# x transposed as it lands, its reciprocal root spread by a diagonal matmul, and the first weight products taken k by k: the start of a hybrid transformer block

## The chip, the cores and the metric

The kernel runs on one core of a Trainium2 chip. The metric is the time of one execution on the device, in microseconds (us), lower is better. The core has TensorE (PE, the matrix engine; PEld is its loading of weights), VectorE (DVE), ScalarE (ACT), GpSimd (POOL) and SyncE (SP, which issues most of the DMAs). Each engine works through a list of its own in order; semaphores between the lists make one wait for another. On-chip data lie in SBUF, 128 partitions wide; matmuls write into PSUM.

## The reference

One layer of a block for 512 latent tokens (x) and 256 context tokens (ctx), each with 1024 channels. Only the first lines of it are touched by the change; the rest is cut to its outline.

```python
mod  = split(silu(c)     @ w_mod + b_mod, 6)          # c: (1, 1024), w_mod: (1024, 6144)
modc = split(silu(c_ctx) @ w_mod + b_mod, 6)
h  = rmsnorm(x,   norm1_g) * (1 + mod[1])  + mod[0]    # rmsnorm: x * rsqrt(mean(x*x) + 1e-6) * g
hc = rmsnorm(ctx, norm1_g) * (1 + modc[1]) + modc[0]
u, uc = split(h @ w_in, ...), split(hc @ w_in, ...)
y = mlstm(u, uc), diff_attention(u, uc), mamba2_ssd(u, uc)   # three branches
x = x + mod[2] * ((sum of sigmoid(gate_b) * (y_b @ w_b)) @ w_out)
x = x + mod[5] * conv_ffn(rmsnorm(x, norm2_g) * (1 + mod[4]) + mod[3])
```

## The kernel before

**Products in three parts.** The matmuls of the projections take numbers in the fp32r form. To keep the precision, each operand is split into hi (the rounded value) and lo (the remainder), and a product is the sum of three: hi x hi, hi x lo, lo x hi. `split` (L170) does it for weights: ScalarE casts hi (L173), then VectorE, or in every third call GpSimd, subtracts to get lo (L85 is the helper `tt` that issues it). `wpiece` (L177) loads 1024 x 128 numbers of a weight into `wr` (two buffers) and splits them into `wh` and `wl` (four buffers each). `proj_part` (L194) issues the matmuls for some of the eight blocks k of 128 channels: per k, three for the latents (512 columns) and, where wanted, three for the context (256 columns). L82 is the helper `mm`, L88 `stt` (two operations on two tensors and a column), L94 `ts` (on one tensor and one or two columns), L104 `act`.

**The start.** c, the norm gains, x and ctx land first (`xs`: six tiles of 128 tokens by 1024 channels). NG (L251) is the copy of the norm gains. Then, for three pairs of token tiles (L256 on): ScalarE squares and sums each (`junk`, `ssq`), VectorE computes the reciprocal root of two columns (`rs`; L121, twelve small operations), scales both tiles of xs by it, and TensorE transposes (L266); the PSUM results are copied into `xT` (channels on partitions, 768 token columns: 256 of the context, then 512 latents), half by VectorE (L270), half by ScalarE.

**The two channel parts.** `h_part(n)` makes h for four of the eight channel blocks. It loads eight pieces `wm` of w_mod (512 KB each, SP's queue, buffers set by `bufs`) and multiplies them by `scl` (the silu of c and c_ctx), four matmuls per piece: a w_mod group. The sum goes to `msb` (L338), TensorE transposes it (L341), VectorE adds the bias to get MT (shift and scale) and makes the columns A = (1 + scale) * norm gain. Then per k, for latents and context: ScalarE writes hi = A * xT + shift (`hl_101`), VectorE the same in full precision into xT in place, and VectorE (even k) or GpSimd (odd k) lo = xT - hi (`hl_102`). `hct` holds both halves for the context.

**The early pieces.** `first` (L372) lists four: the gates' columns (`wgh`, `wgl`), the keys' first piece (C_KM) and two query pieces (C_QM and the next). `early(n)` (L357) issues their matmuls for the four k of part n, piece after piece. `run` (L151) interleaves two generators in the given ratio as the program is written; the rest of the order comes from a scheduler that follows priorities by that order. After the start come the three branches, the merge and the FFN; their code is the same before and after.

```python
        run(h_part(0))
        with tc.issue_after(last[0].ins):
            for e in first[1:2]:
                e[0] = wcol(e[3])
        for n in range(1, NS):
            run(h_part(n), NK + EX, early(n - 1), KW * (NE + 1))
        run(early(NS - 1))
```

Of the kernel before, what the change touches and what calls it, by code (L numbers as in the profile page):

```python
# [18 lines left out]
P = 128  # L19
D = 1024  # L20
# [18 lines left out]
def build(tc, a, out):  # L39
# [44 lines left out]
    def tt(eng, o, x, y, op):  # L84
        eng.tensor_tensor(out=o, in0=x, in1=y, op=op)  # L85
# [129 lines left out]
    NS, NE, EX = 2, 3, 3  # L215
# [14 lines left out]
    with pool("ph0", 1) as p0:  # L230
# [25 lines left out]
        for i in range(3):  # L256
            for t in (2 * i, 2 * i + 1):
                junk = p0.tile([P, D], mybir.dt.bfloat16, tag="junk", name="junk", bufs=1)
                act(junk, xs[:, t, :], AF.Square, accum=ssq[:, t:t + 1])
            rstd(rs[:, 2 * i:2 * i + 2], ssq[:, 2 * i:2 * i + 2], 2, 1.0 / D)  # L260
            for t in (2 * i, 2 * i + 1):
                ts(V, xs[:, t, :], xs[:, t, :], rs[:, t:t + 1])
            for k in range(0, NK, 2):
                tp = pss()
                for n in range(4):
                    PE.transpose(out=tp[:, n * P:(n + 1) * P], in_=xs[:, 2 * i + n % 2, (k + n // 2) * P:(k + n // 2 + 1) * P],  # L266
                                 identity=ident)
                o = xT[:, k:k + 2, i * 256:(i + 1) * 256]
                if k % 4:
                    V.tensor_copy(o, tp.rearrange("p (k c) -> p k c", k=2))  # L270
                else:
                    S.copy(o, tp.rearrange("p (k c) -> p k c", k=2))

# [48 lines left out]
        split(wgh, wgl, wg)  # L322
        def h_part(n):
# [10 lines left out]
            if n == 0:  # L334
                pt(0)
# [14 lines left out]
            for k in range(n * KW, (n + 1) * KW):  # L350
                for r, cs, h_ in ((0, slice(TC, NT), hlat), (1, slice(0, TC), hctx)):
                    hins[0] = act(h_[0][:, k, :], xT[:, k, cs], AF.Identity, scale=A1[:, k, r:r + 1], bias=MT[:, 0, k, r:r + 1])
                    ts(V, xT[:, k, cs], xT[:, k, cs], A1[:, k, r:r + 1], MT[:, 0, k, r:r + 1], ALU.mult, ALU.add)
                    tt(G if k % 2 else V, h_[1][:, k, :], xT[:, k, cs], h_[0][:, k, :].bitcast(F32), ALU.subtract)
            yield

        def early(n):  # L357

            for i, e in enumerate(first):
                if n == 0 and i:  # L360
                    for e_ in first[i + 1:i + 2]:
                        with tc.issue_after(last[0].ins):
                            e_[0] = wcol(e_[3])
                if n == 0:
                    e[1] = (psl if e[4] else pss)()
                    e[2] = (psl if e[4] else pss)() if e[5] else None
                for k in range(n * KW, (n + 1) * KW):
                    with tc.issue_after(last[1].ins) if n < NS - 1 else ExitStack():
                        proj_part(e[0], e[1], e[2], range(k, k + 1))
                    yield  # L370

        first = [[(wgh, wgl), None, None, 0, True, True], [None, None, None, C_KM, True, True],  # L372
                 [None, None, None, C_QM, False, False], [None, None, None, C_QM + P, False, False]][0:NE + 1]
        hins = [None]
        run(h_part(0))
        with tc.issue_after(last[0].ins):
            for e in first[1:2]:
                e[0] = wcol(e[3])
        for n in range(1, NS):
            run(h_part(n), NK + EX, early(n - 1), KW * (NE + 1))  # L380
        run(early(NS - 1))
# [7 lines left out]
        with tc.issue_after(hins[0].ins):  # L389
            act(gcol[:, 5:6], gcol[:, 1:2], AF.Exp)  # L390
# [880 lines left out]
```

## Time and profile before

| | us |
|---|---|
| median of 3 runs | 1126.54 (1126.38 to 1129.1) |
| the profiled execution | 1129.0 |
| its span in the trace | 1127.2 |
| TensorE busy | 1080.3 (96%) |
| VectorE busy | 720.9 (64%) |
| ScalarE busy | 472.8 (42%) |
| GpSimd busy | 282.7 (25%) |

The mean granted clock of TensorE is 0.989 of its full speed. All times in the rows below are microseconds from the start of the span of that one execution. Matmuls follow each other in a pipeline, so the time in a row of one matmul overlaps with that of the next; what a matmul costs in a dense stretch is the distance between the starts.

### The profile page before, as it was taken

To read this page: it belongs to the slowest core of one execution; us is meant where nothing else is said; L and a number is where in the kernel's file an instruction comes from. 1 tells how busy PE (TensorE), PEld (TensorE's weight loads), DVE (VectorE), ACT (ScalarE), POOL (GpSimd) and SP (SyncE) were. 2 spreads that over 40 slices of the span, in tenths; PEclk is the share of its full clock that TensorE was granted. 3 is DMA by queue.
4 is the path that set the end of the run, shared out by engine and by line. 5 is a ranking of instruction groups with operands and counts; after the bars stand their busy time and mean duration, and the time that the engine had idled before them with its cause. 6 is when DMAs were issued, how large, how long until landed. Compare 5 with 4: busy or idle time off the path is not lost.

```text
span 1127.2 us, 16645 instructions
## 1 busy us (share of the span) xinstructions
PE 1080.3 (96%) x6402; PEld 943.8 (84%) x6402; DVE 720.9 (64%) x1351; ACT 472.8 (42%) x885; POOL 282.7 (25%) x243
## 2 busy tenths in 40 slices
PE   4898999999999999999998999989999999999998
PEld 3587899988888998789987887988888888888887
DVE  6577678669645783976685647687876656651311
ACT  5456444556324333246635363333543344431110
POOL 3230001035325732630331002243221212111110
PEclk9999999999999999999998899999999999999999
DMA  8722322236425363330316112424433333322321
GB/s 295 238 59 61 97 72 57 76 89 165 130 84 175 99 179 93 91 94 20 76 31 194 57 57 86 139 72 153 150 112 100 90 108 92 97 94 94 131 94 38
DMA packets 139951, 119.41 MB, mean 106 GB/s; under 512 B 7009, under 2 KB 115912, under 8 KB 139872
## 3 DMA queue, kind: packets, MB, share of 16 engines
q1 hardware_dynamic: 139248, 118.02, 34.6%
q8 instruction: 50, 0.82, 0.3%
q0 software_dynamic: 624, 0.33, 0.3%
q14 instruction: 29, 0.24, 0.1%
HBM read 116.10 MB, written 2.23 MB: 105 GB/s over the span
## 4 chain that ended last, share of the span: by engine, by line
PE 79%; DVE 10%; ACT 3%; DMA 3%; issue 2%; POOL 2%; SPq 0%; DVEq 0%; ACTq 0%; POOLq 0%
PE pl L82 56%; PE psx L82 18%; DVE t L85 2%; PE sc L82 2%; DVE t L88 2%; DVE wl L85 1%; ACT t L104 1%; PE pl L944 1%; DMA wm<-in_w_mod_dram 1%; POOL t L85 1%; ACT wh L173 1%; POOL wl L85 1%; DMA xs<-in_ctx_dram 1%; PE psx L266 1%; DVE rs L85 0%
## 5 line engine op out<-in xcount | busy, mean ns | idle before, releaser
L85 POOL TENSOR_TENSOR wl<-wr,wh 128x1024 fp32r<-128x1024 f32 x59 | 145.1, 2459 | 621.8 <-ACT wh L173 543.5
L173 ACT CAST wh<-wr 128x1024 fp32r<-128x1024 f32 x150 | 157.6, 1051 | 276.3 <-PE pl L82 169.0
L82 PE MATMUL pl<-h,wh 128*128 128x512 f32 (+1 forms) x768 | 223.0, 374 | 3.7 <-DVE ft L88 2.5
L85 DVE TENSOR_TENSOR wl<-wr,wh 128x1024 fp32r<-128x1024 f32 x91 | 116.3, 1279 | 155.4 <-ACT wh L173 154.5
L82 PE MATMUL pl<-hl,wh 128*128 128x512 f32 x608 | 200.3, 398 | 1.2 <-ACT sga L104 0.8
L82 PEld LDWEIGHTS pl<-h,wh 128*128 128x128 f32 x768 | 141.3, 190 | 29.5 <-issue 3.1
L82 PE MATMUL pl<-wh,hl 128*128 128x256 f32 x768 | 148.7, 288 | 3.0 <-ACT t L649 3.0
L82 PE MATMUL pl<-h,wl 128*128 128x512 f32 (+1 forms) x384 | 142.8, 373 | 0.0
L82 PEld LDWEIGHTS pl<-hl,wh 128*128 128x128 f32 x608 | 113.2, 189 | 24.8 <-issue 1.3
L82 PEld LDWEIGHTS pl<-wh,hl 128*128 128x128 f32 x768 | 121.8, 191 | 4.0 <-ACT t L649 3.2
L82 PE MATMUL pl<-hl,wl 128*128 128x512 f32 x304 | 120.3, 396 | 0.0
L82 PE MATMUL pl<-wl,hl 128*128 128x256 f32 x384 | 109.5, 286 | 0.0
L82 PEld LDWEIGHTS pl<-h,wl 128*128 128x128 f32 x384 | 72.9, 190 | 12.4
L82 PEld LDWEIGHTS pl<-wl,hl 128*128 128x128 f32 x384 | 73.3, 191 | 0.6 <-issue 0.2
L88 DVE SCALAR_TENSOR_TENSOR ft<-pl,PT,ft 128x511 f32<-128x511 f32 x88 | 65.3, 744 | 5.5 <-ACT ft L104 4.2
L82 PEld LDWEIGHTS pl<-hl,wl 128*128 128x128 f32 x304 | 57.4, 189 | 11.5
L82 PE MATMUL psx<-wh,ah 128*128 128x512 f32 (+1 forms) x176 | 66.5, 379 | 0.0
L82 PE MATMUL psx<-wl,ah 128*128 128x512 f32 (+1 forms) x176 | 66.2, 376 | 0.0
L82 PE MATMUL psx<-wh,al 128*128 128x512 f32 (+1 forms) x176 | 66.2, 376 | 0.0
L85 DVE TENSOR_TENSOR al<-ft,ah 128x512 fp32r<-128x512 f32 x22 | 45.5, 2069 | 31.3 <-ACT ah L173 31.3
L82 PE MATMUL pl<-y,wh 128*128 128x512 f32 x192 | 60.2, 395 | 0.7 <-DVE t L88 0.5
L82 PE MATMUL psx<-wh,t 128*128 128x256 f32 x256 | 46.5, 282 | 1.8 <-POOL t L85 1.0
(311 smaller groups left out, 2006.4 us busy)
## 6 DMA issues: line engine op xcount, KB each, us to landing
wr<-in_w_in_dram SPq DMA_DIRECT2D x64, 512.0 KB, 4.3
wr<-in_w_up_dram SPq DMA_DIRECT2D x44, 512.0 KB, 3.7
t<-in_w_mod_dram SPq DMA_DIRECT2D x48, 256.0 KB, 4.6
wr<-in_w_down_dram SPq DMA_DIRECT2D x22, 512.0 KB, 3.6
wm<-in_w_mod_dram SPq DMA_DIRECT2D x16, 512.0 KB, 6.0
t<-nmd SPq DMA_DIRECT2D x24, 256.0 KB, 4.8
wr<-in_w_out_dram SPq DMA_DIRECT2D x8, 512.0 KB, 3.5
fc<-in_w_mod_dram SPq DMA_DIRECT2D x16, 256.0 KB, 4.8
```

What stands on the lines that cost most here:

```text
L82: return PE.matmul(o, l, r, start=start, stop=stop)
L85: eng.tensor_tensor(out=o, in0=x, in1=y, op=op)
L88: V.scalar_tensor_tensor(out=o, in0=x, scalar=sc, in1=y, op0=op0, op1=op1)
L104: return S.activation(o, x, f, **kw)
L173: S.copy(hi, src)
L266: PE.transpose(out=tp[:, n * P:(n + 1) * P], in_=xs[:, 2 * i + n % 2, (k + n // 2) * P:(k + n // 2 + 1) * P], identity=ident)
L944: PE.transpose(out=tp[:, t * P:(t + 1) * P], in_=p0[:, (t0 + t) * P:(t0 + t + 1) * P], identity=ident)
```

## The change

The three rounds of reciprocal root and scaling are gone. TensorE transposes xs as it landed and VectorE copies all twelve PSUM tiles out. ScalarE's squares run beside it, and one reciprocal root is taken over all six columns. `dg` holds six diagonal matrices (the identity times a column of rs each, 768 columns); a matmul of ones with `dg` puts the roots of all tokens into every partition of PSUM (`rsp`: 512 columns for the latents, 256 for the context), and ScalarE copies them to SBUF (`rsb`). In `h_part`, VectorE now makes xT * A * root in one operation (the root from PSUM in part 0, from SBUF in part 1), ScalarE adds the shift to get hi, and VectorE makes lo = (xT + shift) - hi; GpSimd has no lo any more. `pt(0)`, which transposes the bias rows, moves ahead of the root. The weights' DMA (`load`) and their split (`ready`) are apart, and the keys' split is put behind the second hi. `early` takes gates and keys together, k by k, then the two query pieces. The parameter loads and the gates' split, which stood behind the transposes, stand ahead of them.

```diff
-        for i in range(3):
-            for t in (2 * i, 2 * i + 1):
-                junk = p0.tile([P, D], mybir.dt.bfloat16, tag="junk", name="junk", bufs=1)
-                act(junk, xs[:, t, :], AF.Square, accum=ssq[:, t:t + 1])
-            rstd(rs[:, 2 * i:2 * i + 2], ssq[:, 2 * i:2 * i + 2], 2, 1.0 / D)
-            for t in (2 * i, 2 * i + 1):
-                ts(V, xs[:, t, :], xs[:, t, :], rs[:, t:t + 1])
-            for k in range(0, NK, 2):
-                tp = pss()
-                for n in range(4):
-                    PE.transpose(out=tp[:, n * P:(n + 1) * P], in_=xs[:, 2 * i + n % 2, (k + n // 2) * P:(k + n // 2 + 1) * P],
-                                 identity=ident)
-                o = xT[:, k:k + 2, i * 256:(i + 1) * 256]
-                if k % 4:
-                    V.tensor_copy(o, tp.rearrange("p (k c) -> p k c", k=2))
-                else:
-                    S.copy(o, tp.rearrange("p (k c) -> p k c", k=2))
...
+        for i in range(3):
+            for t in (2 * i, 2 * i + 1):
+                junk = p0.tile([P, D], mybir.dt.bfloat16, tag="junk", name="junk", bufs=1)
+                act(junk, xs[:, t, :], AF.Square, accum=ssq[:, t:t + 1])
+            for k in range(0, NK, 2):
+                tp = pss()
+                for n in range(4):
+                    PE.transpose(out=tp[:, n * P:(n + 1) * P], in_=xs[:, 2 * i + n % 2, (k + n // 2) * P:(k + n // 2 + 1) * P],
+                                 identity=ident)
+                V.tensor_copy(xT[:, k:k + 2, i * 256:(i + 1) * 256], tp.rearrange("p (k c) -> p k c", k=2))
+        pt(0)
+        rstd(rs, ssq, 6, 1.0 / D)
+        dg = p0.tile([P, 6, P], F32, name="dg")
+        tt(V, dg, ident.unsqueeze(1).broadcast_to([P, 6, P]), rs.unsqueeze(2).broadcast_to([P, 6, P]), ALU.mult)
+        rsp = [pss(), pss()]
+        mm(rsp[0], ones.broadcast_to([P, P]), dg[:, 2:6, :].rearrange("p t c -> p (t c)"))
+        mm(rsp[1][:, 0:TC], ones.broadcast_to([P, P]), dg[:, 0:2, :].rearrange("p t c -> p (t c)"))
+        rsb = p0.tile([P, NT], F32, name="rsb")
+        S.copy(rsb[:, TC:NT], rsp[0])
+        S.copy(rsb[:, 0:TC], rsp[1][:, 0:TC])
...
-            if n == 0:
-                pt(0)
...
             for k in range(n * KW, (n + 1) * KW):
                 for r, cs, h_ in ((0, slice(TC, NT), hlat), (1, slice(0, TC), hctx)):
-                    hins[0] = act(h_[0][:, k, :], xT[:, k, cs], AF.Identity, scale=A1[:, k, r:r + 1], bias=MT[:, 0, k, r:r + 1])
-                    ts(V, xT[:, k, cs], xT[:, k, cs], A1[:, k, r:r + 1], MT[:, 0, k, r:r + 1], ALU.mult, ALU.add)
-                    tt(G if k % 2 else V, h_[1][:, k, :], xT[:, k, cs], h_[0][:, k, :].bitcast(F32), ALU.subtract)
-            yield
+                    rb = rsb[:, cs] if n else rsp[r][:, 0:cs.stop - cs.start]
+                    stt(xT[:, k, cs], xT[:, k, cs], A1[:, k, r:r + 1], rb, ALU.mult, ALU.mult)
+                    hins.append(act(h_[0][:, k, :], xT[:, k, cs], AF.Identity, bias=MT[:, 0, k, r:r + 1]))
+                    stt(h_[1][:, k, :], xT[:, k, cs], MT[:, 0, k, r:r + 1], h_[0][:, k, :].bitcast(F32), ALU.add, ALU.subtract)
+                if k % 2:
+                    yield
+
+        def load(e):
+
+            r = wp.tile([P, 1024], F32, tag="wr", name="wr", bufs=2).rearrange("p (k c) -> p k c", c=P)
+            nc.sync.dma_start(r, w_in.rearrange("(k p) c -> p k c", p=P)[:, :, e[3]:e[3] + P])
+            e[0] = r
+
+        def ready(e):
+            lo = wp.tile([P, 1024], F32R, tag="wl", name="wl", bufs=4).rearrange("p (k c) -> p k c", c=P)
+            hi = wp.tile([P, 1024], F32R, tag="wh", name="wh", bufs=4).rearrange("p (k c) -> p k c", c=P)
+            split(hi, lo, e[0])
+            e[0] = (hi, lo)
...
         def early(n):
 
-            for i, e in enumerate(first):
-                if n == 0 and i:
-                    for e_ in first[i + 1:i + 2]:
-                        with tc.issue_after(last[0].ins):
-                            e_[0] = wcol(e_[3])
+            ks = range(n * KW, (n + 1) * KW)
+            if n == 0:
+                for e in first[0:2]:
+                    banks(e)
+            for k in ks:
+                for e in first[0:2]:
+                    proj_part(e[0], e[1], e[2], range(k, k + 1))
+                    yield
+            for e in first[2:]:
                 if n == 0:
-                    e[1] = (psl if e[4] else pss)()
-                    e[2] = (psl if e[4] else pss)() if e[5] else None
-                for k in range(n * KW, (n + 1) * KW):
-                    with tc.issue_after(last[1].ins) if n < NS - 1 else ExitStack():
-                        proj_part(e[0], e[1], e[2], range(k, k + 1))
+                    with tc.issue_after(last[0].ins):
+                        load(e)
+                    ready(e)
+                    banks(e)
+                for k in ks:
+                    proj_part(e[0], e[1], e[2], range(k, k + 1))
                     yield
 
         first = [[(wgh, wgl), None, None, 0, True, True], [None, None, None, C_KM, True, True],
-                 [None, None, None, C_QM, False, False], [None, None, None, C_QM + P, False, False]][0:NE + 1]
-        hins = [None]
-        run(h_part(0))
+                 [None, None, None, C_QM, False, False], [None, None, None, C_QM + P, False, False]]
+        hins = []
+        hp0 = h_part(0)
+        for _ in range(NK):
+            next(hp0)
         with tc.issue_after(last[0].ins):
-            for e in first[1:2]:
-                e[0] = wcol(e[3])
-        for n in range(1, NS):
-            run(h_part(n), NK + EX, early(n - 1), KW * (NE + 1))
-        run(early(NS - 1))
+            load(first[1])
+        next(hp0)
+        with tc.issue_after(hins[1].ins):
+            ready(first[1])
+        e0 = early(0)
+        for _ in range(3):
+            next(e0)
+        run(hp0)
+        run(h_part(1), NK + 2, e0, 13)
+        run(early(1))
```

TensorE at the start of the program, before: L266 are the transposes of xs, the names `pl_289` the sum of the w_mod groups of part 0, `prm` the parameter rows of `pt(0)`, `msb` the modulation of part 0.

```order
L266 MATMUL psx<-ident,xs 128x128 x16
L82 MATMUL pl_289<-wm,scl 32x256 x12
L266 MATMUL psx<-ident,xs 128x128 x16
L82 MATMUL pl_289<-wm,scl 32x256 x8
L266 MATMUL psx<-ident,xs 128x128 x3
L82 MATMUL pl_289<-wm,scl 32x256 x4
L266 MATMUL psx<-ident,xs 128x128 x13
L82 MATMUL pl_289<-wm,scl 32x256 x4
L315 MATMUL psx<-ident,prm 128x128
L82 MATMUL pl_289<-wm,scl 32x256 x4
L341 MATMUL psx<-ident,msb 128x128 x2
```

The same place after the change; `dg,ones` are the two spreading matmuls.

```order
L314 MATMUL psx<-ident,xs 128x128 x48
L82 MATMUL pl_269<-wm,scl 32x256 x20
L297 MATMUL psx<-ident,prm 128x128
L82 MATMUL psx<-dg,ones 128x512
L82 MATMUL psx<-dg,ones 128x256
L82 MATMUL pl_269<-wm,scl 32x256 x12
L344 MATMUL psx<-ident,msb 128x128 x2
```

All 48 transposes now stand ahead of the first w_mod group; five groups follow in one piece, and three stand behind the spreading matmuls.

VectorE from the bias copy on, before: PT is the transposed bias, MT the modulation columns, A_85 the scale columns; operations on `hl_102` and on `hct` with three names are lo.

```order
L316 COPY PT<-psx 128x128
L85 TENSOR_TENSOR MT<-psx,PT 128x2x2 x4
L88 SCALAR_TENSOR_TENSOR A_85<-MT,NG 128x8
L85 TENSOR_TENSOR wl<-wr,wh 128x1024
L94 TENSOR_SCALAR xT<-xT,A_85,MT 128x512
L94 TENSOR_SCALAR xT<-xT,A_85,MT 128x256
L85 TENSOR_TENSOR hl_102<-xT,hl_101 128x512
L94 TENSOR_SCALAR xT<-xT,A_85,MT 128x512
L85 TENSOR_TENSOR hct<-xT,hct 128x256
```

VectorE at that place after the change, beginning with the diagonals.

```order
L85 TENSOR_TENSOR dg<-ident,rs 128x768
L298 COPY PT<-psx 128x128
L85 TENSOR_TENSOR MT<-psx,PT 128x2x2 x4
L88 SCALAR_TENSOR_TENSOR A_85<-MT,NG 128x8
L88 SCALAR_TENSOR_TENSOR xT<-xT,A_85,psx 128x512
L88 SCALAR_TENSOR_TENSOR xT<-xT,A_85,psx 128x256
...
L88 SCALAR_TENSOR_TENSOR xT<-xT,A_85,psx 128x512
L88 SCALAR_TENSOR_TENSOR xT<-xT,A_85,psx 128x256
L88 SCALAR_TENSOR_TENSOR hl_102<-xT,MT,hl_101 128x512
L88 SCALAR_TENSOR_TENSOR hct<-xT,MT,hct 128x256
L85 TENSOR_TENSOR wl<-wr,wh 128x1024
```

The weight split and the first lo have changed places, and all eight scalings of the part stand ahead of the first lo.

TensorE around the transposes of the second part's modulation, before: `pl_388` and `pl_389` are the gates' sums for latents and context, `pl_432` and `pl_433` the keys', `psx` from hl the query pieces'; L315 transposes the later parameter rows (`pt(1)`, `pt(2)`).

```order
L82 MATMUL psx<-hl_101,wl 128x512
L341 MATMUL psx<-ident,msb 128x128 x2
L82 MATMUL psx<-hl_101,wh 128x512
L82 MATMUL psx<-hl_102,wh 128x512
...
L82 MATMUL psx<-hl_102,wh 128x512
L82 MATMUL psx<-hl_101,wl 128x512
L315 MATMUL psx<-ident,prm 128x128 x2
L82 MATMUL pl_388<-hl_101,wgh 128x512
L82 MATMUL pl_432<-hl_101,wh 128x512
```

The same place after the change, where `pl_346` and `pl_347` are the gates' sums and `pl_348` and `pl_349` the keys'.

```order
L82 MATMUL psx<-hl_101,wl 128x512
L344 MATMUL psx<-ident,msb 128x128 x2
L297 MATMUL psx<-ident,prm 128x128 x2
L82 MATMUL pl_346<-hl_101,wgh 128x512
L82 MATMUL pl_348<-hl_101,wh 128x512
L82 MATMUL psx<-hl_101,wh 128x512 x2
L82 MATMUL pl_347<-hct,wgh 128x256
L82 MATMUL pl_349<-hct,wh 128x256
L82 MATMUL pl_346<-hl_102,wgh 128x512
```

Twelve matmuls of the fourth piece's part 0 stood behind the two transposes of msb; now all of the part 0 matmuls stand ahead of them, and the matmuls on part 1's h follow.

## Rows read from the trace of the kernel before

**Rows 1.** The page's first part: busy time, share of the span and instructions.

```profile
PE 1080.3 (96%) x6402; PEld 943.8 (84%) x6402; DVE 720.9 (64%) x1351; ACT 472.8 (42%) x885; POOL 282.7 (25%) x243
```

**Rows 2.** Windows: busy (count) of PE, PEld, DVE, ACT, POOL; clock; DMA; GB/s.

```profile
19.00:20.00 1.00, 1.00 (x17) 0.56 (x20) 0.95 (x5) 0.08 (x1) 0.00 (x0) 1.00 0.51 195
20.00:21.00 1.00, 1.00 (x19) 0.49 (x8) 1.00 (x2) 0.00 (x0) 0.00 (x0) 1.00 0.06 10
...
33.00:33.50 0.50, 0.50 (x6) 0.07 (x6) 0.50 (x2) 0.50 (x2) 0.00 (x0) 0.53 1.13 338
36.00:36.50 0.50, 0.50 (x9) 0.20 (x8) 0.50 (x2) 0.30 (x1) 0.39 (x1) 0.56 0.91 299
36.50:37.00 0.50, 0.50 (x9) 0.21 (x2) 0.50 (x2) 0.50 (x1) 0.00 (x0) 1.00 0.94 360
86.00:87.00 1.00, 0.00 (x0) 0.00 (x0) 0.00 (x0) 0.99 (x2) 0.00 (x0) 1.00 0.21 63
```

**Rows 3.** Timeline to 30: start, time, engine, operation, count, [idle before <- releaser].

```profile
11.21 0.17 DVE L251 COPY NG<-psx 128x16 f32<-128x16 f32 x1 [2.71 <-ACT scl L104]
12.24 0.17 DVE L94 TENSOR_SCALAR rs<-ssq 128x2 f32<-128x2 f32 x1 [0.86 <-ACT junk L104]
...
14.42 0.16 DVE L88 SCALAR_TENSOR_TENSOR rs<-rs,rs 128x2 f32<-128x2 f32 x1
...
19.03 1.65 PE L82 MATMUL pl<-wm,scl 128*32 128x256 f32 x24
...
25.76 1.46 DVE L270 COPY xT<-psx 128x512 f32<-128x512 f32 x2 [0.77 <-PE psx L266]
...
28.63 0.37 ACT L338 COPY msb<-pl 128x256 f32<-128x256 f32 x1 [1.96 <-PE pl L82]
...
29.82 0.15 DVE L88 SCALAR_TENSOR_TENSOR A<-MT,NG 128x8 f32<-128x8 f32 x1
```

**Rows 4.** Timeline from 34 to 89: the places that decide when TensorE goes on.

```profile
34.48 0.80 PE L82 MATMUL pl<-hl,wgh 128*128 128x512 f32 x1
...
51.57 0.38 PE L341 MATMUL psx<-ident,msb 128*128 128x128 f32 x2
...
52.27 0.16 DVE L88 SCALAR_TENSOR_TENSOR A<-MT,NG 128x8 f32<-128x8 f32 x1
...
65.78 0.27 PE L82 MATMUL pl<-hct,wl 128*128 128x256 f32 x1
...
88.87 0.39 PE L82 MATMUL pl<-wh,hl 128*128 128x256 f32 x1 [3.04 <-ACT t L649]
```

**Rows 5.** Timeline of TensorE: starts of matmuls that follow each other.

```profile
42.75 0.64 PE L82 MATMUL psx<-wm,scl 128*32 128x256 f32 x8
43.32 0.50 PE L82 MATMUL pl<-hl,wh 128*128 128x512 f32 x1
...
59.27 0.28 PE L82 MATMUL pl<-hct,wh 128*128 128x256 f32 x1
59.39 0.40 PE L82 MATMUL pl<-hl,wgh 128*128 128x512 f32 x1
59.62 0.40 PE L82 MATMUL pl<-hl,wgl 128*128 128x512 f32 x1
```

**Rows 6.** Groups by form: busy, mean ns; or min/mean/max ns and from when.

```profile
L88 DVE SCALAR_TENSOR_TENSOR t<-t,scl,t x48: 731/744/2857, 258.5 to 652.5; 128x512 f32<-128x512 f32 x48
L88 DVE SCALAR_TENSOR_TENSOR t<-pl,PT,t 128x255 f32<-128x255 f32 x20 | 9.4, 468 | 2.0 <-ACT t L104 1.9
L85 DVE TENSOR_TENSOR hl<-xT,hl 128x512 fp32r<-128x512 f32 x4 | 2.7, 681 | 0.0
L85 DVE TENSOR_TENSOR wl<-wr,wh 128x1024 fp32r<-128x1024 f32 x4 | 4.9, 1225 | 7.1 <-ACT wh L173 7.1
L82 PE MATMUL psx<-t,ones x4: 591/592/595, 305.2 to 358.1; 128*128 128x512 f32 x4
```

**Rows 7.** Timeline near 887: GpSimd and VectorE, both with two SBUF inputs.

```profile
886.82 2.40 POOL L85 TENSOR_TENSOR wl<-wr,wh 128x1024 fp32r<-128x1024 f32 x1 [8.48 <-ACT wh L173]
887.30 2.48 DVE L85 TENSOR_TENSOR al<-ft,ah 128x512 fp32r<-128x512 f32 x1 [1.88 <-ACT ah L173]
```

More of the change, by code (lines that the diff above doesn't have):

```diff
@@ L213, in proj_w @@
         return pre.pop(c0) if c0 in pre else proj_cm(wcol(c0), lat, ctxt)
-    NS, NE, EX = 2, 3, 3
+    NS = 2
     W = D // NS
@@ new lines, in ready, with banks @@
+        def ready(e):
[3 more added lines that the diff above has]
+            e[0] = (hi, lo)
+        def banks(e):
+            e[1] = (psl if e[4] else pss)()
+            e[2] = (psl if e[4] else pss)() if e[5] else None
+        def early(n):
+            ks = range(n * KW, (n + 1) * KW)
[7 more added lines that the diff above has]
+            for e in first[2:]:
+                if n == 0:
+                    with tc.issue_after(last[0].ins):
[4 more added lines that the diff above has]
+                    proj_part(e[0], e[1], e[2], range(k, k + 1))
@@ L388, in build @@
         V.tensor_copy(gcol[:, 0:5], PT[:, 2, R3_G:R3_G + 5])
-        with tc.issue_after(hins[0].ins):
+        with tc.issue_after(hins[-1].ins):
             act(gcol[:, 5:6], gcol[:, 1:2], AF.Exp)
```

## The prediction, made before the changed kernel was run

> **What bounds the kernel now.** The page's first part puts TensorE at 96% of the span [rows 1], so what the change can move is where TensorE idles, runs slowly or waits: the start, the only place that the diff touches. I read the start in the order of time (the timeline), then the same stretch cut into short windows for clock and DMA, then the waits behind it. Three things stand out. TensorE's first matmul on h lo comes at 34.48 [rows 4]; before it the scale columns A of the first channel part are ready at 29.97 [rows 3]. Between 19 and 21 the DMA engines nearly stop (195 and 10 GB/s) [rows 2]: five w_mod buffers are full and wait for TensorE. And from 33.0 to 36.4 the granted clock is 0.5, its lower level of 1.2 GHz, after a stretch in which TensorE had mostly idled; it is full again from 36.5 [rows 2]. Then TensorE is busy without a gap to the last matmul of the keys (C_KM), at 65.78, and on to 85.8. There it idles 3.04 us until 88.87 [rows 4], waiting for ScalarE; the chain of waits leads from there back through a cast, a split and a load of a later weight piece to the end of the keys, which frees that piece's buffer. So the one number that carries to the end is when the keys are done: 65.78 + 0.27 = 66.05.
>
> I walk the new order to that number. The trace is one of 1129.0 us (span 1127.2, the rest 1.8 lies outside); the median of the runs shown is 1126.54, 2.5 lower. The sum is a difference to that trace, put on the median.
>
> **1. To the scale columns of part 0.** Removed: three reciprocal roots one after another, six scalings of xs, and the split of the drains over two engines. The transposes now need only the landed x; VectorE drains all twelve. It starts after the NG copy, at 11.38, as ScalarE's order up to there is unchanged. Twelve drains at 0.73 (two took 1.46) make 8.8: 20.1. One root of twelve small operations, as before (12.24 to 14.58, 2.3): 22.5 [rows 3]. The diagonal has 768 elements, two inputs: between 0.68 for 512 and 1.23 for 1024 [rows 6], I take 0.95: 23.4. The two spreading matmuls are not in the trace; the nearest is the 512-column spread by ones, two records of 0.59 each [rows 6]. For 512 and 256 columns together that bounds them at 0.9 (records fully overlapped) and 1.8 (not at all); I take 1.3, as other records overlap: 24.7. TensorE's list has three w_mod groups queued behind them, 1.65 for three [rows 3]: 26.4. From there to A, before needs 28.63 to 29.97 plus the semaphore, 1.4: A at **27.8**, 2.2 earlier. The loads cover this: five groups run in one piece when the transposes end (eight drains, 17.2, plus some 0.6), so loads 6 to 8 are issued from about 18.3 and the hole of 19 to 21 closes. If the last of them is late, A is 0.6 later.
>
> **2. To the first lo.** All eight scalings of part 0 now stand ahead of the first lo on VectorE. None of that form (two tensors and a column) is new in kind: 0.74 for 512 [rows 6], 0.47 for 256; four of each are 4.8 end to end, 4.2 if neighbours overlap by 0.08; I take 4.4. With a lo of 0.74 TensorE starts at **33.0** instead of 34.48, 1.5 earlier. ScalarE's hi casts lie inside: its first starts after one scaling, and the weight split that stood before it is moved behind. GpSimd's lo operations fall away; that costs VectorE 4 x (0.74 + 0.47) but ends its own stalls beside GpSimd.
>
> **3. To the second transposes of the modulation.** From here TensorE is the limit, and its list decides. Spacings: 0.23 for 512 columns, 0.12 for 256, and 0.7 for a w_mod group (0.57 from the group to the next matmul, plus the gap at its edges) [rows 5]. Before: 35 of 512, 23 of 256 and 6 groups from 34.48 to 51.57 [rows 4]: 8.05 + 2.76 + 4.2 = 15.0 of 17.1; of the 2.1 left about 1.0 is the half clock up to 36.4, the rest waits. Now: 46, 22 and 5 groups: 10.6 + 2.6 + 3.5 = 16.7, since two more weight pieces' part 0 stands ahead of these transposes. With the same 2.1: 33.0 + 18.8 = **51.8**. So the 1.5 is spent: 51.8 against 51.57.
>
> GpSimd still splits one weight piece here, beside VectorE's lo of k = 2 and 3. A two-input VectorE operation beside such a split took 2.48, the split 2.40 [rows 7]; alone its kind takes 0.68 [rows 6]. So the lo of k = 2 comes some 2 later, near 39.3, and TensorE has about 6 us of matmuls between the first lo and that one, so it arrives at 39 too: I cost it at nothing, and at 1 if that cover is thinner. The Trainium skill, "GPSIMD Engine Reference", section 1 (Specifications), says the same: its SBUF interfaces are shared with VectorE and contend when VectorE has two SBUF inputs. The trace agrees (2.48 against 0.68); a reader who ignored it would have the lo of k = 2 at 37 and the same sum, but with 2 us of slack.
>
> **4. To the keys' end.** Before, twelve matmuls of the fourth piece still stand behind the second transposes (12 x 0.23 = 2.8); they cover the 0.9 to the new A (51.57 to 52.43) [rows 4] and the first hi and lo, so TensorE never waits. Now nothing stands there. From 51.8: 0.9 to A plus 0.3 for a small copy put between: 53.0; eight scalings 4.4: 57.4; another copy 0.3 and the lo of k = 4, 0.74: 58.5. Until then TensorE has only four matmuls of 512 and two of 256 that need no lo, 1.2 us; it idles about 5 of 6.7 us in two waits. Behind them stand 28 of 512 and 22 of 256: 6.4 + 2.6 = 9.1, and the later lo are done by 63, before they are wanted. Keys done at **67.6**, against 66.05: 1.5 later.
>
> **5. Behind the keys.** Sixteen matmuls of the early pieces are left instead of twelve, 0.9 more for TensorE, but it waits 3.04 at 85.83 for the chain from the keys, so that is hidden: 88.3 against a release of 88.87 + 1.5 = 90.4. The 1.5 is carried to the end. Further back the two orders differ only in how neighbours interleave; nothing prices that, and I allow 2 either way.
>
> Sum: -2.2 at A, +0.7 for the scalings (-1.5 at the first lo), +1.7 for the longer list up to the second transposes (+0.2), +1.3 for the waits less the work moved ahead: **+1.5**, so 1126.5 + 1.5 = **1128.0** (1130.5 for an execution like the profiled one). That is 0.13%, below the 0.3% (3.4 us) that a measurement of this kernel can tell from no change.
>
> **Rivals.**
> *The early start carries (faster).* If TensorE finds work in the waits of step 4, because A comes well before it reaches the transposes' end or the scalings overlap more than I think, the keys end when the work does: 33.0 + (46 + 32) x 0.23 + (22 + 24) x 0.12 + 3.5 + 2.1 + 0.5 for the transposes = 62.6, or 61.6 without the half clock: 3.4 to 4.4 earlier, **1122.6**. For it speaks that TensorE is 96% busy and all this work is the same. Against it: every engine takes its list in order, and the list has no matmul free of lo there. It decides if the two waits together are under 1 us.
>
> *The clock falls in the waits (slower).* In step 4 TensorE idles 5 of 6.7 us, and 9.1 us of dense matmuls follow. In the trace an idle stretch before 33.0 was followed by 3.4 us at half clock, worth 1.7; at 85.8 a wait of 3.04 was not (clock 1.00) [rows 2, 4]. Should the clock be down for 7 of the 9.1 us at full-clock pace, they cost up to 3.5 more: 1128.0 + 3.5 = **1131.5**. It decides from 3.8 us at half clock on (1.9 lost). The Trainium skill, "TensorE: Matmul & The Clock Gate", Part 1, has an idle TensorE at half rate until sustained activity releases it; by that rule the fall would come. The two rows disagree among themselves, so I give it less than even.
>
> *The start is not what counts.* If the 3.04 at 85.8 hangs on something that doesn't move with the keys (the gates' own chain through ScalarE's logarithms), an earlier or later end of the keys vanishes, up to 3: **1126.5**. The gates' sums end about 1 us before the keys in either order, so it would look the same: no change.
>
> **How the numbers follow.** Forecast 0.5; the start doesn't count 0.1; early start carries 0.18; clock 0.22. The first two lie within 0.3% but for the interleaving behind (2 either way), which takes 0.02 to each side; of the clock case a fifth stays within. Faster 0.2, same 0.58, slower 0.22. The range runs from the fast rival to the slow one with half of the unpriced 2: 1122.6 to 1132.
>
> **What would show it.** Right: the DMA hole at 19 to 21 gone; drains back to back from 11.4 to 20; A of part 0 near 27.8; first lo matmul near 33; second transposes near 52; then two idle pieces of TensorE, together near 5 us, and the keys done at 67 to 68; the wait at 88 shortened to 2. Wrong: no idle after the second transposes, or a granted clock of 0.5 behind them for several us; A of part 0 later than 29 (drains or the spread dearer); or a new wait of over 2 us behind 118 us, where the lists only interleave anew.

## The result and the profile after

The changed kernel takes 1136.74 us (median of 6 executions, 1133.58 to 1140.51) against 1126.88 before: a ratio of 1.0081, 95% interval 1.0062 to 1.0101. By the medians it is slower by 9.9 us, where 1128.0 and no measurable change were forecast; the time lies above the range. The profiled execution took 1136.85 us with a span of 1133.9. That of before (1129.0) is 2.1 us above this median of before, so its span of 1127.2 shows only 6.7 of the difference.

The page's first part after the change:

```profile
PE 1086.6 (96%) x6406; PEld 947.0 (84%) x6406; DVE 721.2 (64%) x1336; ACT 469.5 (41%) x881; POOL 276.2 (24%) x235
```

Windows of the changed kernel (columns as in [rows 2]):

```profile
19.00:20.00 1.00, 0.64 (x8) 0.16 (x8) 0.83 (x6) 0.00 (x0) 0.00 (x0) 1.00 1.05 399
20.00:21.00 1.00, 0.62 (x9) 0.21 (x9) 0.86 (x5) 0.00 (x0) 0.00 (x0) 1.00 1.02 395
57.00:58.00 1.00, 0.81 (x2) 0.72 (x3) 1.00 (x3) 0.98 (x2) 0.00 (x0) 0.50 0.00 0
59.00:60.00 1.00, 1.00 (x4) 0.74 (x3) 1.00 (x6) 0.10 (x1) 0.00 (x0) 0.50 0.00 0
91.00:92.00 1.00, 1.00 (x5) 1.00 (x6) 1.00 (x3) 0.21 (x2) 0.00 (x0) 0.50 0.08 16
93.00:94.00 1.00, 1.00 (x7) 1.00 (x6) 0.97 (x2) 0.00 (x0) 0.00 (x0) 0.50 0.00 0
```

The hole in the DMA is closed (399 and 395 GB/s where [rows 2] have 195 and 10). The granted clock is at its lower level near 57 to 60 and again near 91 to 94; in the kernel before it was full in both places, behind the wait at 86 too [rows 2]. Windows of the kernel before:

```profile
57.00:58.00 1.00, 1.00 (x7) 0.78 (x5) 1.00 (x3) 0.98 (x2) 0.77 (x2) 1.00 0.00 0
91.00:92.00 1.00, 1.00 (x11) 1.00 (x10) 0.97 (x3) 0.00 (x0) 0.00 (x0) 1.00 0.06 16
```

Timeline of the changed kernel up to the first lo:

```profile
11.16 7.26 DVE L316 COPY xT<-psx 128x512 f32<-128x512 f32 x12
...
18.34 0.16 DVE L94 TENSOR_SCALAR rs<-ssq 128x6 f32<-128x6 f32 x1
...
20.75 0.96 DVE L85 TENSOR_TENSOR dg<-ident,rs 128x768 f32<-128x768 f32 x1
...
21.85 1.53 PE L82 MATMUL psx<-dg,ones 128*128 128x512 f32 x4 [0.57 <-DVE dg L85]
...
26.26 0.16 DVE L88 SCALAR_TENSOR_TENSOR A<-MT,NG 128x8 f32<-128x8 f32 x1
26.53 4.29 DVE L88 SCALAR_TENSOR_TENSOR xT<-xT,A,psx 128x512 f32<-128x512 f32 x8
...
28.65 0.64 PE L82 MATMUL psx<-wm,scl 128*32 128x256 f32 x8 [2.71 <-DMA wm<-in_w_mod_dram]
...
30.74 0.75 DVE L88 SCALAR_TENSOR_TENSOR hl<-xT,MT,hl 128x512 fp32r<-128x512 f32 x1
...
32.93 0.50 PE L82 MATMUL pl<-hl,wgh 128*128 128x512 f32 x1
```

Timeline of TensorE from the second transposes on, at the rows that answer to [rows 4], and its further waits up to 401:

```profile
50.86 0.38 PE L344 MATMUL psx<-ident,msb 128*128 128x128 f32 x2
...
53.51 0.50 PE L82 MATMUL pl<-hl,wgh 128*128 128x512 f32 x1 [1.47 <-ACT hl L104]
...
57.19 0.79 PE L82 MATMUL pl<-hl,wgh 128*128 128x512 f32 x1 [2.25 <-DVE hl L88]
...
67.56 0.28 PE L82 MATMUL pl<-hct,wl 128*128 128x256 f32 x1
...
90.93 0.58 PE L82 MATMUL pl<-wh,hl 128*128 128x256 f32 x1 [2.36 <-ACT t L682]
...
120.36 1.13 PE L82 MATMUL psx<-t,kw 128*128 128x130 f32 x8 [0.64 <-DVE kw L92]
...
236.54 0.85 PE L789 MATMUL pl<-ident,t 128*128 128x128 f32 x6 [1.30 <-DVE sm L88]
264.80 0.70 PE L82 MATMUL psx<-xw,t 128*128 128x256 f32 x2 [0.92 <-POOL xw L85]
278.15 0.87 PE L789 MATMUL pl<-ident,t 128*128 128x128 f32 x6 [1.46 <-ACT t L790]
...
400.45 1.10 PE L82 MATMUL psx<-t,t 128*128 128x64 f32 x8 [0.94 <-DVE t L85]
```

The kernel before at the last five places (it has no wait at the first L756 group, near 230):

```profile
118.00 1.13 PE L82 MATMUL psx<-t,kw 128*128 128x130 f32 x8 [1.55 <-DVE kw L92]
...
257.92 0.70 PE L82 MATMUL psx<-xw,t 128*128 128x256 f32 x2 [0.20 <-POOL xw L85]
271.66 0.88 PE L756 MATMUL pl<-ident,t 128*128 128x128 f32 x6 [0.94 <-ACT t L757]
272.91 0.73 PE L82 MATMUL pl<-hl,wh 128*128 128x512 f32 x2 [0.37 <-ACT t L757]
...
394.43 1.10 PE L82 MATMUL psx<-t,t 128*128 128x64 f32 x8 [0.93 <-DVE t L85]
```

Read the two side by side as a lag. The last matmul of the keys starts 1.8 later (67.56 against 65.78), the wait for ScalarE ends 2.1 later (90.93 against 88.87), the kw matmul (the first on `kw`, at 118.00 and 120.36) 2.4 later. So behind the lower clock from 91 to 94 the lag has grown by 0.3 only: the kw matmul waits 0.64 where it had waited 1.55, and that hides most of the loss. Then comes what the prediction had no price for: from the kw matmul to the wait near 400 the kernel before needs 276.43 us and the changed one 280.09, 3.7 more, in code that the change does not touch. The waits there account for 2.2 of it (1.30 + 0.92 + 1.46 against 0.20 + 0.94 + 0.37). From 400 to the end the order of TensorE's list is the same in both kernels but for single records, and the lag grows only from 6.0 to 6.7.

So two theories stood against each other. **S**: all of it follows from the start, the late keys and the half clock behind the waits. **L**: a part comes from the later list of TensorE, which the scheduler interleaves in another way. (The lists of the other engines behind the start are laid out anew with it, so "the list" below stands for the whole layout; no run tells which engine's order costs the time.)

### The profile page after: what moved, and what is told of

It is laid out like the page before. It is cut to its first block, busy times and chain, and to the rows that moved or that the text cites. A ratio compares the mean times of both kernels' runs of the same rounds, so it can differ in the third digit from the quotient of the medians.

```text
span 1133.9 us, 16621 instructions
## 1 busy us (share of the span) xinstructions
PE 1086.6 (96%) x6406; PEld 947.0 (84%) x6406; DVE 721.2 (64%) x1336; ACT 469.5 (41%) x881; POOL 276.2 (24%) x235
## 4 chain that ended last, share of the span: by engine, by line
PE 73%; DVE 10%; issue 2%; POOL 2%; ACT 2%; DMA 1%; SPq 0%; DVEq 0%; ACTq 0%
PE pl L82 52%; PE psx L82 17%; PE sc L82 2%; DVE t L85 2%; DVE t L88 2%; POOL t L85 1%; DVE wl L85 1%; DMA t<-nmd 1%; PE pl L977 1%; ACT wh L173 0%; DVE sm L88 0%; DVE h L85 0%; DVE sm L896 0%; DVE zacc L85 0%; DVE sga L88 0%
```

## The experiments

Medians in us; the ratio is to the kernel before on the same chip. "Keys" is the start of the last keys matmul, "kw to 400" the distance just read (276.43 in the kernel before; a dash where the list begins in another order), both from the profiled execution.

| kernel | median | ratio (95%) | keys | kw to 400 |
|---|---|---|---|---|
| changed (first time) | 1136.74 | 1.0081 (1.0062 to 1.0101) | 67.56 | 280.09 |
| e4 changed, again | 1136.97 | 1.0076 (1.0051 to 1.0101) | 67.43 | 280.01 |
| e1 cover of 12 | 1129.89 | 1.0029 (1.0010 to 1.0048) | 62.64 | 279.66 |
| e2 cover of 12, other list | 1127.86 | 1.0006 (0.9989 to 1.0023) | 63.83 | 276.57 |
| e3 cover of 22 | 1124.28 | 0.9971 (0.9955 to 0.9988) | 61.96 | - |
| e5 transposes alone | 1126.35 | 0.9995 (0.9974 to 1.0016) | 63.26 | 275.83 |
| e6 early pieces alone | 1129.17 | 1.0010 (0.9992 to 1.0027) | 69.76 | - |
| e7 before, no cover | 1128.79 | 1.0017 (1.0000 to 1.0034) | 64.76 | - |
| e8 lo sooner | 1128.92 | 1.0011 (0.9995 to 1.0026) | 67.37 | - |
| e9 cover and lo sooner | 1123.74 | 0.9976 (0.9960 to 0.9992) | 61.98 | - |
| e10 waits filled (28) | 1129.88 | 1.0031 (1.0016 to 1.0046) | 66.82 | 276.42 |
| e11 filled a little (8) | 1128.89 | 1.0021 (1.0009 to 1.0034) | 66.35 | 276.58 |
| e12 filled (8), the changed list | 1134.55 | 1.0069 (1.0054 to 1.0085) | 69.27 | 280.42 |

The last column splits by order. From the kw matmul to 400 the kernel before, e2, e10 and e11 have the same order on all five engines, but for single records, and take 276.42 to 276.58. The changed kernel, e4, e1 and e12 have another, again the same on all five engines, with some 250 of TensorE's 1778 records elsewhere, and take 279.66 to 280.42. The wait of 1.30 near 236 stands in these four profiles and in none of the other ten. e5 has a third order.

**e1 to e4: cover behind the second transposes, with different later lists.** Cover is work that TensorE can do where it would wait: here matmuls on part 0, which the call of `run` fills in between the steps of `h_part(1)`. The edit is one number or two, which leave part of them behind the transposes:

```diff
-        run(h_part(1), NK + 2, e0, 13)
+        run(h_part(1), NK + 8, e0, 13)    # e1
+        run(h_part(1), NK + 4, e0, 13)    # e2
+        run(h_part(1), NK + 6, e0, 10)    # e3
```

> One number changed against the changed kernel: the fill of the second channel part is spread over 16 steps instead of 10, so that twelve matmuls of 512 columns on part 0 stand behind the second modulation's transposes, as in the kernel before. The list of TensorE from the keys on is that of the changed kernel up to its row 3288. Theory S (the loss arises at the start: two waits of 1.47 and 2.25 us and the half clock behind them, and once more behind the wait at 88): the twelve matmuls (2.8) take the place of one wait, keys done near 65 instead of 67.84, TensorE no longer at half clock near 57 or near 91, total 1136.7 - 2.8 - 1.7 - 1.7 = 1130.5, and from 118 to 284 the lead or lag against the kernel before changes by less than 1. Theory L (a part arises later, because the scheduler interleaves the matmuls between 118 and 284 in another way): the keys come earlier in the same way, but between 118 and 284 this kernel still loses 3 to 4 us against the kernel before, as the changed kernel did (2.4 behind at 118, 6.1 at 284).

> The same with 12 steps instead of 10: again twelve matmuls behind the second transposes, the start as in the run before, but the later list of TensorE stands nearer to that of the kernel before (82 matmuls moved against it, 279 against the changed kernel). Theory S: the same time as the other kernel with twelve matmuls, within 1 us. Theory L: the 3 to 4 us between 118 and 284 go, so 2 to 4 us less than that kernel: 1126.5 to 1128.5.

> 14 steps and a fill of 10: 22 matmuls of part 0 stand behind the second transposes, and the later list of TensorE is that of the kernel before from 460 matmuls behind the keys on (57 moved in all). Theory S: both waits are covered (22 x 0.23 = 5.1), the keys are done near 63, 3 earlier than before, total 1123.5 to 1125, and 1.5 to 4 less than with twelve. Theory L: the same start, and no loss between 118 and 284, so that it is 5 to 8 less than the kernel with twelve matmuls and the changed kernel's later list, 1123.

> The changed kernel once more, on the chip on which the other three run, to compare with them: 1136.7, within 2 either way by both theories; the keys done at 67.8 and the release at 91, if its first profile is typical, with half clock behind each of the two waits in most executions.

In e1 the two waits became one of 2.07, and the keys came 5 us sooner than in the changed kernel. It leads the kernel before by 1.9 at the kw matmul and has lost that lead, and 1.3 more, at 400. Timeline of e1:

```profile
53.62 0.50 PE L82 MATMUL pl<-hl,wgh 128*128 128x512 f32 x1 [2.07 <-DVE hl L88]
...
116.09 1.13 PE L82 MATMUL psx<-t,kw 128*128 128x130 f32 x8 [1.28 <-DVE kw L92]
...
395.75 1.10 PE L82 MATMUL psx<-t,t 128*128 128x64 f32 x8 [0.95 <-DVE t L85]
```

The start is repaired and 3.2 us are lost behind it all the same, with the changed kernel's list: L. But e1's total, 1129.89, is near S's 1130.5 too, though the lower clock behind the wait at 86 stayed (0.50 from 87 to 90). On this one chip the kernel before takes 1126.18, e1 1129.89 and the changed kernel (e4) 1136.97. e1 and e4 share the later list, so 7.1 hang on the start and the clock, more than on the list: both theories hold a part. e2 lies 2.0 below e1 with the keys 1.2 later, as L has it, though the two intervals overlap. e3 has the cover and the other list, and beats the kernel before. e4 repeats the changed kernel.

**e5 and e6: one half of the change each.** e5 has the changed order of the parameter loads, the transposes, the root and the scalings, with the old loading of the weights, the old `early` and the old call:

```diff
-        run(hp0)
-        run(h_part(1), NK + 2, e0, 13)
-        run(early(1))
+        run(h_part(0))
...
+        for n in range(1, NS):
+            run(h_part(n), NK + EX, early(n - 1), KW * (NE + 1))
+        run(early(NS - 1))
```

e6 is the kernel before with the changed `early`, `load`, `ready`, `banks` and that call in place of its own, and a yield behind every second block in `h_part`.

> The changed kernel's load, transposes, spread root and scalings, with the early pieces one after the other as in the kernel before: twelve matmuls stand behind the second transposes. Its later list of TensorE is a third one (179 moved against before, 324 against the changed kernel). Theory S (all is decided by the end of the keys and the clock there): the start as in the runs with twelve matmuls behind, release near 86 instead of 88.87, total 1126.2 - 2.9 + 1.7 for a half clock = 1125. Theory L (the list between 118 and 284 costs by itself): the time at the first matmul behind 284 differs from what the lead at 118 gives by more than 1, either way; total 1122 to 1129.

> The kernel before with the early pieces alone taken as in the change (gates and keys k by k, load and split apart). No matmul stands behind the second transposes, but VectorE's list has the first lo behind two scalings, not eight. Theory S: first lo near 34.5 as before, second transposes 2.8 later, near 54.4, then waits of about 0.9 and 1.0, keys near 68, 1.9 later than before: 1128, and 1130 if the clock falls there. Theory L: the same start, and up to 4 more or less between 118 and 284, since 136 matmuls of the later list stand elsewhere.

Neither half alone is measurably slower. e5's keys are 2.5 earlier than before and bring nothing that can be measured; its time is 1.4 above S's figure and inside L's wide range, so it doesn't tell them apart. Of its lead, 2.5 at the end of the wait for ScalarE (86.33), nothing is left at the kw matmul (117.96), behind a wait of 1.66. In e6 both waits behind the second transposes are short (0.40 and 0.83), but the transposes themselves start at 55.76, 1.4 later than expected, after a stretch of lower clock (0.50 from 31 on, 0.69 from 37 to 38), and the keys come at 69.76 instead of 68. The total is that of theory S; the list neither added nor took. The keys end 4.0 later than before and the total is at most 0.27% (3.0 us) higher: not all of a later end of the keys comes through to the end.

**e7 and e8: what makes the waits.** e7 changes one number of the kernel before; e8 changes VectorE's list in the changed kernel.

```diff
-    NS, NE, EX = 2, 3, 3
+    NS, NE, EX = 2, 3, 0              # e7
```

```diff
+            los = []
...
-                    stt(xT[:, k, cs], xT[:, k, cs], A1[:, k, r:r + 1], rb, ALU.mult, ALU.mult)
+                    with tc.issue_after(los[-3].ins) if n and len(los) > 2 else ExitStack():
+                        stt(xT[:, k, cs], xT[:, k, cs], A1[:, k, r:r + 1], rb, ALU.mult, ALU.mult)
...
+                    los.append(...the lo of this block...)    # e8
```

> The kernel before with one number changed (EX 3 to 0), so that all matmuls of part 0 stand ahead of the second transposes and none behind them. Theory S: the cover is what matters: two waits appear in the kernel before as well, together 2 to 3, the keys come 2 later, total 1128 to 1130. Theory L: the same, and the later list (120 moved, and not the changed kernel's) adds or takes up to 4. If neither wait appears, the cover was not what the kernel before lived on.

> The changed kernel, with VectorE's list in part 1 changed so that the lo of a block stands behind three scalings instead of eight. Still no matmul behind the second transposes. Theory S: the second wait (2.25, for the first lo) goes or falls below 0.5, the first (1.47, for the first hi) stays; the clock need not fall near 57; keys 65 to 66 instead of 67.8; total 1137 - 2 - 0 to 3.4 = 1131.5 to 1135. Theory L: the later list is another one (354 moved against the changed kernel, 184 against before), so the loss between 118 and 284 may be gone, for 1128 to 1131.

e7's total lies where it was expected, but the way there doesn't: without cover the kernel before waits only 0.40 and 0.83, where its first lo stands behind two scalings, and the keys come 1.0 sooner than before, not 2 later (its profile has no lower clock near 33). The long second wait needs the eight scalings. e8 shows the same from the other side. VectorE's timeline in e8, up to the first lo of part 1, which in the changed kernel came at 56.39:

```profile
51.98 1.81 DVE L88 SCALAR_TENSOR_TENSOR xT<-xT,A,rsb 128x512 f32<-128x512 f32 x3
53.71 0.28 DVE L298 COPY PT<-psx 128x128 f32<-128x128 f32 x1
53.91 0.74 DVE L360 SCALAR_TENSOR_TENSOR hl<-xT,MT,hl 128x512 fp32r<-128x512 f32 x1
```

The second wait is gone. Yet the keys end no sooner (67.37): behind the first wait the clock was down from 54 on (0.56, 0.50 and 0.50 in the three windows to 57), with TensorE busy throughout. With the keys where the changed kernel has them, e8 takes 8 us less; only its later list and the clock are others.

**e9: both cures.** e3's call and e8's scalings, these in both parts (`if len(los) > 2`).

> The two cures together: 22 matmuls of part 0 behind the second transposes, and the first lo of each part behind three scalings instead of eight; the later list stands near that of the kernel before (55 moved). Theory S: as the kernel with 22 matmuls alone (1124.3), less at most 0.7 at the first lo of part 0, since no wait was left in part 1: 1123 to 1125. Theory L: the same, as that list is the same from 460 matmuls behind the keys on.

As expected: no wait is left in part 1, and 0.24% less than before (0.08 to 0.40). e3's interval overlaps with it.

**e10 to e12: TensorE kept busy in the waits.** Extra matmuls write columns 256 to 511 of the keys' context sum, which nothing reads:

```diff
         run(early(1))
...
+        with tc.issue_after(tlast[0].ins):         # tlast: second transposes; e10: 12, e12: 8
+            for _ in range(12):
+                mm(first[1][2][:, 256:512], wgh[:, 0, :], hctx[0][:, 0, :], False, False)
...
+                    if dum[0] and k == 4 and n == 0 and w is not first[0][0]:   # e10: 16, e11: 8
+                        dum[0] = 0
+                        with tc.issue_after(z.ins):
+                            for _ in range(16):
+                                mm(pc[:, 256:512], wgh[:, 0, :], hctx[0][:, 0, :], False, False)
```

> The changed kernel with 28 extra matmuls of 256 columns that nothing reads, 12 in the first wait behind the second transposes and 16 in the second (1.4 and 1.9 us at 0.12 each, so that they end before the wait would): TensorE keeps busy there, and nothing that is needed comes sooner. The later list is a new one (266 moved against the changed kernel). Theory S: only the clock can gain: if it stays full near 57, the keys come at 66.2 instead of 67.8 and the total is 1137 - 1.7, with the second fall near 91 gone another 1.7: 1133.5 to 1135.5. Theory L: the loss between 118 and 284 goes with the list, another 3 to 4: 1130 to 1132. The claim that the clock falls because TensorE idles is wrong if it still falls near 57.

> The same with only 8 such matmuls, in the second wait (1.0 of 2.25 us); TensorE's list behind them is, row for row, that of the run with 28. Theory S: the waits stay, the clock falls near 57 as in the changed kernel, so 1137 within 1, and 2 to 4 more than the run with 28. Theory L: the keys as in the changed kernel (67.4 to 67.8) and yet 3 to 4 less in total, 1133, since only the later list differs.

> The changed kernel with 8 such matmuls in the first wait (1.0 of 1.87 us); here TensorE's later list is, row for row, that of the changed kernel. Theory S and theory L alike: 1137 within 1 if the clock still falls near 57; 1133.5 to 1135.5 if the shorter idle time keeps it up. Beside the run with 8 in the second wait it differs in the later list alone: theory L has it 3 to 4 slower than that one, theory S equal within 1.

e11 and e12 are the cleanest pair. They have the same start but for where the eight small matmuls and a few neighbours stand, and ran on the same chip. Timeline of e11, then of e12:

```profile
119.71 1.13 PE L82 MATMUL psx<-t,kw 128*128 128x130 f32 x8 [0.75 <-DVE kw L92]
...
396.29 1.11 PE L82 MATMUL psx<-t,t 128*128 128x64 f32 x8 [0.93 <-DVE t L85]
```

```profile
122.62 1.13 PE L82 MATMUL psx<-t,kw 128*128 128x130 f32 x8 [0.99 <-DVE kw L92]
...
239.13 0.85 PE L793 MATMUL pl<-ident,t 128*128 128x128 f32 x6 [1.30 <-DVE sm L88]
...
403.04 1.10 PE L82 MATMUL psx<-t,t 128*128 128x64 f32 x8 [0.93 <-DVE t L85]
```

e12 needs 280.42 from kw to 400, e11 276.58: 3.8 more with the changed kernel's list, with its wait at 239 again. The medians differ by 5.7. In this pair of profiles the rest arises at the start, where e12's keys come 2.9 later, with a longer stretch of lower clock, as the windows show. (Behind 400 some 70 matmuls stand elsewhere too; there e12 makes up 0.6.) First e11, then e12:

```profile
57.00:58.00 1.00, 0.92 (x4) 0.79 (x5) 1.00 (x4) 1.00 (x1) 0.00 (x0) 1.00 0.00 0
```

```profile
57.00:58.00 1.00, 0.66 (x2) 0.57 (x3) 1.00 (x3) 1.00 (x1) 0.00 (x0) 0.50 0.00 0
62.00:63.00 1.00, 1.00 (x4) 0.82 (x4) 0.00 (x0) 0.00 (x0) 0.37 (x3) 0.50 0.11 1
```

With eight matmuls in the second wait the clock stayed full and the keys came at 66.35, 1.1 to 1.2 sooner than in the changed kernel; with eight in the first wait it was down until 63 and they came at 69.27. So the fall near 57 is worth 1.1 or more. It is no theory of the whole, though: e10, with both waits filled down to 0.43 and 0.54 and the clock full near 57, was not faster than e11, and the clock still fell near 91 in both. S's figures for e10 (1133.5 to 1135.5) and e11 (1137) are refuted, and for e12 that it would equal e11 within 1. L gave 3 to 4 between e11 and e12, and 3.8 were found from kw to 400; but it had e11 at 1133, 4 too high, since it too counted on the fall near 57. Both theories had e12 at 1137 within 1 if the clock fell; it fell, and e12 took 1134.55.

## Why the prediction failed, point by point

**Steps 1 and 2** were right in their times, with compensating errors. A of part 0 was ready at 26.42, not 27.8: twelve drains took 7.26, not 8.8, and the others hold (root from 18.34, diagonal 0.96 against 0.95, spread 1.53 against 1.3). The first lo was done at 31.49, but TensorE reached it at 32.93 (33.0 forecast), as it waited 2.71 for a w_mod piece that landed no sooner and then ran at the lower clock. That the two agree is luck. The expected slowing of VectorE beside GpSimd's split didn't come (below); it had been costed at nothing.

**Step 3**: second transposes at 50.86, 51.8 forecast. The 2.1 of lower clock and waits that were carried over from before were too much: the clock was down from 29 to 33 here (0.68 to 0.50), ahead of the first lo, and full from 33 on.

**Step 4** had the mechanism and the size: two waits, 1.47 and 2.25 (and 0.40 ahead of them), together 4.1 against "about 5". The keys were done at 67.84, 67.6 forecast, and that is luck: TensorE went on from the second wait at 57.19, 1.3 sooner than forecast, and then took 10.65 for work priced at 9.1, since in this sum stood no half clock. Without it the keys would have been done 1.1 or more sooner (e11). The second wait comes from the eight scalings ahead of the lo (e8), as step 4 had it.

**Step 5** fails. The release, "88.87 + 1.5 = 90.4", was right to 0.5 (90.93). What failed is the sentence behind it: "Further back the two orders differ only in how neighbours interleave; nothing prices that, and I allow 2 either way". That list costs 3.7 between the kw matmul and 400: 279.66 to 280.42 in the four profiles that have it, 276.42 to 276.58 in the four that have the order of the kernel before. By itself this would still lie within the range (1128.0 + 3.7 = 1131.7); with the clock it does not. Nor does "The 1.5 is carried to the end" hold as a rule: of e5's lead nothing is left at the kw matmul, and e6's keys come 4.0 later for 3.0 at most.

**The rival "the clock falls in the waits"** was right that it falls near 57, which was given less than even. Its price was too high there (up to 3.5; 1.1 to 1.2 measured by e11, 1.5 by the 10.65 against 9.1), and it missed that the clock would fall more often: near 91, which in the kernel before had not come behind a longer wait, and elsewhere (below). The Trainium skill, "TensorE: Matmul & The Clock Gate", Part 1, lets the number of slow matmuls vary from one run of a kernel to the next. The executions agree (0.981 to 0.992 granted to the changed kernel), so a single profile of before was a weak ground for a price.

**The early start carries** only once the waits are covered: e3 and e9 take 1124.3 and 1123.7, where this rival had 1122.6. Of the signs of being wrong, the lower clock behind the waits came. A new wait of over 2 us behind 118 did not: the longest is 1.46, so that sign was too coarse for the loss that it was to catch. The chances and the range are also added up wrongly by their own terms, which give 0.2, 0.6 and 0.2 for faster, same and slower, and 1121.6 to 1132.5; nothing hangs on it.

The sum, then. In the two profiles the lag is 6.7: 2.4 at the kw matmul, where 1.5 had been forecast for the keys (the fall near 57 is 1.1 or more of it), 3.7 from the list, 0.7 behind 400. The other 3 of the 9.9 are not in this pair, and as an estimate they go with the clock. Executions with the same granted clock differ by 6 to 7: at 0.989 two of the changed kernel average 1133.88 and thirteen of the kernel before 1127.85; at 0.986 it is 1136.85 in one against 1129.82 in nine. And the changed kernel was granted less, 0.9835 in the median of twelve executions against 0.990 over 93. Where the lower stretches lie differs from one profile to the next. Apart from the last matmuls, the changed kernel's profile has 31 us of them: 29 to 33, 57 to 60, 91 to 94, 586 to 589, 620 to 630 and 640 to 647. That of before has 24: 33 to 36, 613 to 623, 634 to 641 and 753 to 757. The profiled execution of e4, the fastest of the changed kernel's twelve (1131.70), has 17, those near 57 and 91 among them. Why the others come and go stays open. That the list's loss comes from the waits named above (2.2 of 3.7) is read from the profiles alone, in all four that have this list; TensorE has no other wait over 0.15 between kw and 400, and where the other 1.5 arises stays open.

## What to carry to other kernels

Where a scheduler lays out the program, an edit at the start is also an edit of everything behind it. Compare the whole list of the bound engine before and after, not only the edited stretch, and try one or two neutral edits that give another list: here nearly the same start with another list differed by 3.8 us from kw to 400, more than the change won in its best form (0.29%, 3.3 us). And keep work that needs nothing new behind a chain of small operations: with 22 such matmuls behind the second transposes, and a later list near that of the kernel before, the same change was faster than the kernel before by 0.29% (0.12 to 0.45).

## What the runs showed of the hardware

The length of one wait didn't tell whether the clock falls. A wait of 3.04 at 86 left it full in the kernel before [rows 2, 4]; 2.36 at 91 was followed by the lower level in the changed kernel; and in e3, a wait of 1.23 was not and one of 1.44 was. In e9 a wait of 1.43 at the same place as that of 1.44 was not. Waits of TensorE in e3 and the windows behind them, then the same for e9:

```profile
85.66 0.38 PE L82 MATMUL pl<-wh,hl 128*128 128x256 f32 x1 [1.23 <-ACT t L682]
103.39 0.91 PE L82 MATMUL psx<-t,on 64*128 64x384 f32 x2 [1.44 <-DVE t L85]
```

```profile
86.00:87.00 1.00, 1.00 (x11) 1.00 (x10) 1.00 (x3) 0.00 (x0) 0.00 (x0) 1.00 0.00 0
105.00:106.00 1.00, 1.00 (x6) 1.00 (x6) 0.95 (x2) 1.00 (x3) 0.00 (x0) 0.50 0.75 261
```

```profile
103.36 0.91 PE L82 MATMUL psx<-t,on 64*128 64x384 f32 x2 [1.43 <-DVE t L85]
```

```profile
105.00:106.00 1.00, 1.00 (x9) 0.95 (x8) 1.00 (x3) 1.00 (x3) 0.00 (x0) 1.00 0.71 242
```

Beside GpSimd's split, the engine that began second slowed. In [rows 7] the split began first, at 886.82, and took 2.40; the VectorE operation took 2.48, against 0.68 for its kind [rows 6]. In the changed kernel the lo began first, at 35.05, and kept its 0.75; the split, 0.04 later, took 3.37. The kind of VectorE operation does not decide: at 418 in the kernel before, one of the lo's kind (two SBUF inputs and a column) began 0.14 behind a split and took 2.86. So the slowing that step 3 expected stayed away because the lo began first. The Trainium skill, "GPSIMD Engine Reference", section 1 (Specifications), names contention with VectorE instructions that have two SBUF inputs, without saying there who pays. In these three pairs of rows it was the one that began second. Rows of the changed kernel, then of the kernel before:

```profile
35.05 0.75 DVE L88 SCALAR_TENSOR_TENSOR hl<-xT,MT,hl 128x512 fp32r<-128x512 f32 x1
35.09 3.37 POOL L85 TENSOR_TENSOR wl<-wr,wh 128x1024 fp32r<-128x1024 f32 x1 [23.21 <-ACT wh L173]
```

```profile
418.30 2.44 POOL L85 TENSOR_TENSOR wl<-wr,wh 128x1024 fp32r<-128x1024 f32 x1 [2.02 <-ACT wh L173]
418.44 2.86 DVE L88 SCALAR_TENSOR_TENSOR t<-t,scl,t 128x512 f32<-128x512 f32 x1
```
